# Dilated attention with all four heads of a block in one unit, placed on a common beat in TensorE's order

## The chip, the cores and the metric

The kernel runs on one core of a Trainium2 chip (trn2). The metric is the device time of one execution in microseconds (us). The engines are TensorE (PE in the profile, its weight loads PEld), VectorE (DVE), ScalarE (ACT), GpSimd (POOL) and SyncE (SP, which issues most DMAs). Each engine works through its own instructions in the order in which the program lists them; semaphores hold it where it needs another's result.

## What is computed

The reference is a trunk of two layers for 1024 tokens of width 1024. In each layer a normalised input is projected into a pooling mixer and into queries, keys and values of 12 heads. The heads form three groups of four, each with its own window and dilation:

```
DIL_PATTERNS = ((128, 1), (512, 4), (2048, 16))
def dilated_window_attention(q, k, v, window, dil):      # one group of four heads
    steps = window // dil
    ...                                   # tokens split by residue mod dil, then into blocks of 128
    s = einsum('brnqhd,brnkhd->brnhqk', qs, kb) * HEAD_DIM ** -0.5    # kb: the block and the one before it
    s = where((dist >= 0) & (dist <= steps) & (ki >= 0), s, -inf)
    m = max(s); e = exp(s - m); l = sum(e)
    o = einsum('brnhqk,brnkhd->brnqhd', e / l, vb); lse = m + log(l)
...
    wts = softmax(stack(lses))            # the three groups are weighed against each other
    h = h + concat([pool_out, attn_out]) @ w_out
    h = h + square(relu(rmsnorm(h) @ w_up)) @ w_down
    h = h + sigmoid(rmsnorm(h) @ w_gate) * (p[i] @ w_ple[i])
```

## The kernel before, in words

Everything is float32. The large products split each operand into a high and a low part in a rounded float32 format (fp32r) and add three products of them; `products` (lines 549, 551 and 553) issues these as matmuls of 128x128 weights and 512 columns. For one tile of the input projection that is 8 x 3 such matmuls for each half of the tokens. The attention's own matmuls are plain fp32.

The program is written as a planner: a `Clock` holds a time `now` and a heap of pieces of work with due times. `products` calls `ck.tick` after each matmul, which moves the time on by 215 ns and runs whatever has come due. So the order of each engine's instructions is fixed when the program is built: attention's matmuls land between the products of the next projection, where the plan's time puts them, and `ck.now +=` books what they are thought to cost.

In each layer, groups 0 and 1 project queries (`in_qk`), keys and values (`in_v`), then call `attend`, whose work is laid over the projections that follow: group 0's over the six tiles of group 1, group 1's over the four query and key tiles of group 2. The halves of queries and keys are rotated by `rot_evac` (VectorE shuffles and multiplies, GpSimd multiplies, VectorE adds), and the weights of each next tile are split on ScalarE and VectorE, in the same stretch. Group 2's attention lies over the pooling tiles and the projection of its values.

`unit` (line 763) is one unit of attention: a block of 128 queries and, for groups 0 and 1, two heads (a pair); for group 2, all four heads. In group 0 every block but the first, and in group 1 every second block, sees 256 keys (called wide here: K is 256, nb is 2); all others see 128 (narrow). Its steps:

1. scores: one matmul for each head into the two PSUM banks of tag "s" (line 783). Head 2p + hh sits in rows 64 hh to 64 hh + 63, so these use half of the array's rows;
2. on VectorE mask and maximum of each head (line 789) and the scaling of the maxima (line 793), on ScalarE the exponential of each head with its sum (line 796);
3. `stats_out`: GpSimd issues a DMA with the block's maxima and sums (line 759);
4. transposes of the exponentials, 128x128 each, into a bank of tag "e" (two banks in all; line 805), and their eviction by VectorE or ScalarE in turn (lines 810, 812);
5. values: one matmul for each head and key block into the one bank of tag "o" (line 819); head hh fills 64 columns of the array. ScalarE evicts the result (lines 825, 828, 831).

Each step yields the planned time to the next; the value step also waits in the plan until the values are there (`vok`). `attend` starts a unit every 3400 ns for groups 0 and 1 (16 units each) and every 2500 ns for group 2 (8 units), each running its own course. An fp32 score or value matmul shows in the trace as two instructions, a transpose as one. `weigh` (line 975) waits in the plan for the units' outputs and multiplies them by the weights of the groups, before the output projection.

Of the kernel before, what the change touches and what calls it, by code (L numbers as in the profile page):

```python
# [116 lines left out]
def body(nc, tc, pools, A, out):  # L117
# [6 lines left out]
    def bank(name, tag, shape=(128, 512)):  # L124
        return ps.tile(list(shape), F32, name=name, tag=tag)
# [495 lines left out]
    def layer(L, hT, norm, tabs):  # L621
# [141 lines left out]
        def unit(g, n, ps_, q, k, vget, o, lag):  # L763

            two = (n > 0) if g == 0 else (n % 2 == 1) if g == 1 else False
            nb = 2 if two else 1
            np_ = len(ps_)
            K = 128 * nb
            if g == 2:
                mk = cst[:, C_MASK[2]:C_MASK[2] + 128]  # L770
            else:
                mk = cst[:, C_MASK[g] + 256 - K:C_MASK[g] + 256]
            heads = [(i, hh, 2 * p + hh) for i, p in enumerate(ps_) for hh in range(2)]
            for p in ps_:
                for t in (q[p], k[p]):
                    for hf in range(2):
                        ck.need((id(t), hf))
            sp = [bank(f"s{g}", "s", (128, np_, K)) for _ in range(2)]
            k0 = (n - nb + 1) * 128
            for i, hh, h in heads:  # L780
                r = slice(64 * hh, 64 * hh + 64)
                p = ps_[i]
                nc.tensor.matmul(sp[hh][:, i], q[p][r, n * 128:n * 128 + 128],  # L783
                                 k[p][r, k0:k0 + K], start=True, stop=True)
            ck.now += 218.0 * nb * np_
            yield 350.0
            sm = blk(f"sm{g}", F32, (128, np_, 2, K))
            for i, hh, h in heads:
                nc.vector.tensor_tensor_reduce(sm[:, i, hh], sp[hh][:, i], mk, 1.0, -3.0e38,  # L789
                                               OP.add, OP.max, ml[g][:, n, h:h + 1])  # L790
            nm = small.tile([128, 2 * np_], F32, name="nm", tag="nm", bufs=6)
            h0 = 2 * ps_[0]
            nc.vector.tensor_scalar(nm, ml[g][:, n, h0:h0 + 2 * np_], -0.125, None, op0=OP.mult)  # L793
            yield 500.0 + 300.0 * nb * np_
            for j, (i, hh, h) in enumerate(heads):
                nc.scalar.activation(sm[:, i, hh], sm[:, i, hh], AF.Exp, bias=nm[:, j:j + 1],  # L796
                                     scale=0.125, accum_out=ml[g][:, n, 4 + h:5 + h])
            yield 900.0 * np_ + 300.0
            if ps_[-1] == 1:
                stats_out(g, n)  # L800
            stats[g] += np_
            ep = bank(f"e{g}", "e", (128, np_, 2, nb, 128))
            for i, hh, h in heads:
                for kb in range(nb):
                    nc.tensor.transpose(ep[:, i, hh, kb], sm[:, i, hh, kb * 128:kb * 128 + 128], ident)  # L805
            ck.now += 107.0 * 2 * nb * np_
            yield 300.0
            et = blk(f"et{g}", F32, (128, np_, 2, nb, 128))
            if (n + ps_[0]) % 2:
                nc.vector.tensor_copy(et, ep)  # L810
            else:
                nc.scalar.activation(et, ep, AF.Copy)
            yield 900.0 + lag
            while not all(vok(g, n, p) for p in ps_):
                yield 500.0
            op = bank(f"o{g}", "o", (128, np_, 128))
            for i, hh, h in heads:
                for kb in range(nb):
                    nc.tensor.matmul(op[64 * hh:64 * hh + 64, i], vget(n - nb + 1 + kb, h),  # L819
                                     et[:, i, hh, kb], start=kb == 0, stop=kb == nb - 1)  # L820
            ck.now += 107.0 * 2 * nb * np_
            yield 300.0
            for i, p in enumerate(ps_):
                if g == 0:
                    nc.scalar.activation(o[p].rearrange("p (r n a) -> p n r a", r=8, n=8)[:, n],
                                         op[:, i].rearrange("p (r a) -> p r a", r=8), AF.Copy)
                elif g == 1:
                    nc.scalar.activation(o[p].rearrange("p (s x a) -> p x s a", s=2, x=8)[:, n],
                                         op[:, i].rearrange("p (s a) -> p s a", s=2), AF.Copy)
                else:  # L830
                    nc.scalar.activation(o[p][:, n * 128:n * 128 + 128], op[:, i], AF.Copy)

        def attend(g, q, k, vget, base, gap, lag=0.0):
            o = [blk(f"o{g}{p}_{L}") for p in range(2)]
            oT[g] = o
            i = 0
            for n in range(8):
                for ps_ in (((0, 1),) if g == 2 else ((0,), (1,))):
                    ck.go(unit(g, n, ps_, q, k, vget, o, lag), ("o", g, n, ps_[-1]), base + gap * i)
                    i += 1  # L840
# [692 lines left out]
```

## Time and profile before

| | us |
|---|---|
| median of 3 runs | 2332.04 |
| lowest and highest | 2331.57, 2335.32 |
| profiled execution | 2332.01 |
| its span, first to last instruction | 2330.2 |
| TensorE busy in it | 2280.8 (98%) |
| VectorE, ScalarE, GpSimd busy | 1677.5, 1014.7, 694.3 |

The busy time of TensorE is no measure of distance from its best: matmuls are pipelined and their ends are modelled, so that a late start need not show as idle time. What a run of instructions costs is read from the starts: how much later the next product starts than it would have. A row of the timeline merges neighbouring instructions of one kind and gives their first start, the time to their last end, and their count.

### The profile page before, as it was taken

The page shows a single profiled execution, that of the slowest core. Times are in us where ns is not written, and L with a number is a line of the kernel's source. Part 1 is how long each engine was busy: PE and PEld are TensorE (multiplying, and loading weights), DVE is VectorE, ACT ScalarE, POOL GpSimd, SP SyncE. Part 2 cuts the span into 40 slices and gives each one's busy share as a digit, 9 for nine tenths or more (in the row PEclk, how much of TensorE's full clock was granted, in tenths as well). Part 3 has the DMA queues.
Part 4 walks back from the last instruction along what each step waited for, and adds up shares of the span by engine and source line. Part 5 has one row for each costly group of instructions (what it writes and reads, how often), then busy time and mean ns, then how long its engine had stood idle before and what let it go on. Part 6 is the DMA issues. An engine that isn't in the chain of part 4 may idle for free.

```text
span 2330.2 us, 30901 instructions
## 1 busy us (share of the span) xinstructions
PE 2280.8 (98%) x11088; PEld 1841.8 (79%) x11088; DVE 1677.5 (72%) x2832; ACT 1014.7 (44%) x2147; POOL 694.3 (30%) x538
## 2 busy tenths in 40 slices
PE   8999999999999999999999999999999999999998
PEld 6767788788887788888887767878888877888888
DVE  7555677787778787886565467688777787787845
ACT  5243543433345444354324345434333443434645
POOL 5111136333332232342221122354333323333322
PEclk9999999999999999999999999999999999999999
DMA  5011133254447745432220111433444575545214
GB/s 181 19 38 28 38 92 109 77 171 153 155 150 257 234 136 164 148 95 70 61 59 19 38 38 39 106 112 117 155 156 157 198 237 179 172 127 169 89 55 136
DMA packets 296369, 275.65 MB, mean 118 GB/s; under 512 B 12476, under 2 KB 224056, under 8 KB 296216
## 3 DMA queue, kind: packets, MB, share of 16 engines
q1 hardware_dynamic: 293624, 270.04, 37.3%
q0 software_dynamic: 2272, 3.61, 0.9%
q8 instruction: 87, 1.43, 0.3%
q14 instruction: 66, 0.54, 0.1%
q10 hardware_dynamic: 320, 0.03, 0.0%
HBM read 200.99 MB, written 72.58 MB: 117 GB/s over the span
## 4 chain that ended last, share of the span: by engine, by line
PE 82%; DVE 8%; DMA 3%; POOL 2%; ACT 2%; issue 2%; SPq 0%; DVEq 0%; ACTq 0%; POOLq 0%
PE X L566 27%; PE Z L566 12%; PE Y L566 7%; PE in L551 6%; PE in L549 6%; PE in L553 5%; PE gt L553 2%; PE gt L551 2%; PE gt L549 2%; PE s L783 2%; PE o L819 2%; DVE wP L1230 2%; DMA wP<-x_d 2%; PE e L805 1%; POOL res L1058 1%
## 5 line engine op out<-in xcount | busy, mean ns | idle before, releaser
L1230 DVE TENSOR_TENSOR wP<-wP 128x512 fp32r<-128x512 f32 x252 | 197.5, 808 | 0.9 <-ACT wP L1228 0.9
L566 PE MATMUL X<-wP,d1p 128*128 128x512 f32 x768 | 186.2, 395 | 10.2 <-DVE acc L1242 9.7
L566 PE MATMUL X<-wP,d0p 128*128 128x512 f32 x768 | 186.2, 395 | 10.0 <-DVE acc L1242 9.5
L566 PE MATMUL X<-xP,u0p 128*128 128x512 f32 x768 | 183.2, 391 | 0.4 <-ACT y L1164 0.4
L566 PE MATMUL X<-xP,u1p 128*128 128x512 f32 x768 | 183.1, 391 | 0.4 <-ACT y L1164 0.4
L566 PEld LDWEIGHTS X<-wP,d0p 128*128 128x128 f32 x768 | 145.5, 191 | 44.4 <-DVE acc L1242 6.9
L566 PEld LDWEIGHTS X<-wP,d1p 128*128 128x128 f32 x768 | 145.4, 190 | 44.6 <-DVE acc L1242 7.2
L566 PEld LDWEIGHTS X<-xP,u0p 128*128 128x128 f32 x768 | 144.6, 189 | 30.9 <-ACT y L1164 0.8
L566 PEld LDWEIGHTS X<-xP,u1p 128*128 128x128 f32 x768 | 144.6, 189 | 30.9 <-ACT y L1164 0.8
L1190 ACT ACTIVATE y<-y 128x1024 f32<-128x1024 f32 x64 | 67.5, 1055 | 211.8 <-DVE y L1187 211.8
L1228 ACT ACTIVATE wP<-wP 128x512 fp32r<-128x512 f32 x252 | 147.3, 617 | 24.6 <-DMA wP<-x_d 22.2
L190 DVE SCALAR_TENSOR_TENSOR wl<-wr,gt,wh 128x128 fp32r<-128x128 f32 (+1 forms) x288 | 119.9, 447 | 38.5 <-ACT wh L196 38.3
L678 POOL TENSOR_TENSOR rot<-rot,s 128x512 f32<-128x512 f32 x48 | 61.4, 1284 | 278.6 <-DVE rot L676 217.6
L1242 DVE TENSOR_TENSOR acc<-acc,X 128x512 f32<-128x512 f32 x128 | 87.4, 683 | 77.9 <-PE X L566 63.8
L796 ACT ACTIVATE sm<-sm,nm 128x128 f32<-128x128 f32 (+1 forms) x192 | 84.5, 442 | 93.3 <-DVE nm L793 93.1
L196 ACT ACTIVATE wh<-wr,gt 128x128 fp32r<-128x128 f32 (+1 forms) x304 | 104.3, 396 | 0.5 <-DMA wr<-in_w_in_dram 0.5
L566 PE MATMUL Z<-xP,u0p 128*128 128x512 f32 x384 | 93.5, 393 | 4.6 <-DVE res L1079 4.6
L566 PE MATMUL Z<-xP,u1p 128*128 128x512 f32 x384 | 93.5, 393 | 4.5 <-DVE res L1079 4.5
L789 DVE CUSTOM_DVE_ANT_0 sm<-s,cst 128x128 f32<-128x128 f32 (+1 forms) x192 | 58.3, 347 | 52.1 <-PE s L783 52.0
L566 PE MATMUL Z<-wP,d0p 128*128 128x512 f32 x384 | 91.9, 389 | 0.0
L566 PE MATMUL Z<-wP,d1p 128*128 128x512 f32 x384 | 91.9, 389 | 0.0
L330 ACT ACTIVATE d0p<-d0s 128x512 fp32r<-128x512 f32 x64 | 40.1, 628 | 111.9 <-PE X L566 65.7
(474 smaller groups left out, 5923.8 us busy)
## 6 DMA issues: line engine op xcount, KB each, us to landing
wP<-x_d SPq DMA_DIRECT2D x252, 256.0 KB, 3.6
x_d<-ys SPq DMA_DIRECT2D x64, 512.0 KB, 3.6
wr<-in_w_in_dram SPq DMA_DIRECT2D x40, 512.0 KB, 4.2
u0r<-in_w_up_dram SPq DMA_DIRECT2D x32, 512.0 KB, 5.1
x_d<-y SPq DMA_DIRECT2D x32, 512.0 KB, 2.8
u1r<-in_w_up_dram SPq DMA_DIRECT2D x32, 512.0 KB, 5.4
d0r<-in_w_down_dram SPq DMA_DIRECT2D x28, 512.0 KB, 5.8
d1r<-in_w_down_dram SPq DMA_DIRECT2D x28, 512.0 KB, 5.9
```

The costliest lines, as they stand in the source:

```text
L190: nc.vector.scalar_tensor_tensor(l[:, k], raw[:, k], gs[k], f(h[:, k]), op0=OP.mult, op1=OP.subtract)
L196: nc.scalar.activation(h[:, k], raw[:, k], AF.Copy, scale=gs[k])
L549: nc.tensor.matmul(p, wh, h[:, cols], start=first and i == 0, stop=False)
L551: nc.tensor.matmul(p, wh, l[:, cols], start=False, stop=False)
L553: nc.tensor.matmul(p, wl, h[:, cols], start=False, stop=last and i == n - 1)
L566: nc.tensor.matmul(p, w[:, a, i], x[:, b], start=first and i == 0 and a == b == 0, stop=i == n - 1 and a == 1, skip_group_check=not first)
L678: nc.gpsimd.tensor_tensor(a, a, tb["s"][:, hs(hf)], op=OP.mult)
L796: nc.scalar.activation(sm[:, i, hh], sm[:, i, hh], AF.Exp, bias=nm[:, j:j + 1], scale=0.125, accum_out=ml[g][:, n, 4 + h:5 + h])
L1190: nc.scalar.activation(y, y, AF.Square)
L1228: nc.scalar.activation(t[:, 0], f(t[:, 1]), AF.Copy)
L1230: nc.vector.tensor_tensor(t[:, 1], f(t[:, 1]), f(t[:, 0]), op=OP.subtract)
L1242: nc.vector.tensor_tensor(a, a, p, op=OP.add)
```

## The change

A unit of groups 0 and 1 takes all four heads of a block, as group 2's does: 8 units for each group instead of 16. `Unit` holds the steps as methods. `beats` issues them: every 5900 ns of plan, one after the other without a product between them, the transposes of the unit made a beat ago, the values of the one made two beats ago, and the scores of a new one; a group has ten beats. Group 2 keeps its 2500 ns; there the transposes are those of two beats ago and stand directly ahead of the new scores, and the values follow on their own (`alone`). For a wide unit the transposes fill both banks of tag "e", evicted one by VectorE and one by ScalarE; a narrow one fills one bank and is evicted once. The maxima of four heads are scaled by one instruction instead of two. `stats_out` is called together with the exponentials instead of 1200 ns of plan later. `weigh` waits for the unit of four heads.

```diff
-        def unit(g, n, ps_, q, k, vget, o, lag):
-            two = (n > 0) if g == 0 else (n % 2 == 1) if g == 1 else False
...
-            yield 900.0 * np_ + 300.0
-            if ps_[-1] == 1:
-                stats_out(g, n)
...
+        class Unit:
+            def __init__(self, g, n, q, k, vget, o):
+                self.g, self.n, self.q, self.k, self.vget, self.o = g, n, q, k, vget, o
+                two = (n > 0) if g == 0 else (n % 2 == 1) if g == 1 else False
+                self.nb = 2 if two else 1
+                self.heads = [(p, hh, 2 * p + hh) for p in range(2) for hh in range(2)]
+                ck.waiting.add(("o", g, n, 1))
+
+            def scores(self):
...
+                self.sp = [bank(f"s{g}", "s", (128, 2, K)) for _ in range(2)]
+                k0 = (n - self.nb + 1) * 128
+                for p, hh, h in self.heads:
+                    r = slice(64 * hh, 64 * hh + 64)
+                    nc.tensor.matmul(self.sp[hh][:, p], self.q[p][r, n * 128:n * 128 + 128],
+                                     self.k[p][r, k0:k0 + K], start=True, stop=True)
+                ck.now += 436.0 * self.nb
+                ck.go(self.softmax(), delay=350.0)
+
+            def softmax(self):
...
+                self.sm = blk(f"sm{g}", F32, (128, 2, 2, K))
+                for p, hh, h in self.heads:
+                    nc.vector.tensor_tensor_reduce(self.sm[:, p, hh], self.sp[hh][:, p], mk, 1.0, -3.0e38,
+                                                   OP.add, OP.max, ml[g][:, n, h:h + 1])
+                nm = small.tile([128, 4], F32, name="nm", tag="nm", bufs=6)
+                nc.vector.tensor_scalar(nm, ml[g][:, n, 0:4], -0.125, None, op0=OP.mult)
+                yield 500.0 + 600.0 * self.nb
+                for p, hh, h in self.heads:
+                    nc.scalar.activation(self.sm[:, p, hh], self.sm[:, p, hh], AF.Exp, bias=nm[:, h:h + 1],
+                                         scale=0.125, accum_out=ml[g][:, n, 4 + h:5 + h])
                 stats_out(g, n)
+                stats[g] += 2
+
+            def turn(self):
+                g, nb = self.g, self.nb
+                self.ep = ([bank(f"e{g}", "e", (128, 2, nb, 128)) for _ in range(2)] if nb == 2 else
+                           [bank(f"e{g}", "e", (128, 2, 2, 1, 128))])
+                self.et = blk(f"et{g}", F32, (128, 2, 2, nb, 128))
+                for p, hh, h in self.heads:
+                    for kb in range(nb):
+                        d = self.ep[p][:, hh, kb] if nb == 2 else self.ep[0][:, p, hh, kb]
+                        nc.tensor.transpose(d, self.sm[:, p, hh, kb * 128:kb * 128 + 128], ident)
+                ck.now += 428.0 * nb
+                ck.go(self.copy(), delay=300.0)
+
+            def copy(self):
+                for p, e in enumerate(self.ep):
+                    d = self.et[:, p] if self.nb == 2 else self.et
+                    if (self.n + p) % 2:
+                        nc.vector.tensor_copy(d, e)
+                    else:
+                        nc.scalar.activation(d, e, AF.Copy)
+                return
+                yield
+
+            def mix(self):
+                g, n, nb = self.g, self.n, self.nb
+                op = bank(f"o{g}", "o", (128, 2, 128))
+                for p, hh, h in self.heads:
+                    for kb in range(nb):
+                        nc.tensor.matmul(op[64 * hh:64 * hh + 64, p], self.vget(n - nb + 1 + kb, h),
+                                         self.et[:, p, hh, kb], start=kb == 0, stop=kb == nb - 1)
+                ck.now += 428.0 * nb
+                ck.go(self.out(op), ("o", g, n, 1), 300.0)
...
-        def attend(g, q, k, vget, base, gap, lag=0.0):
+        def attend(g, q, k, vget, base, gap, late):
             o = [blk(f"o{g}{p}_{L}") for p in range(2)]
             oT[g] = o
-            i = 0
-            for n in range(8):
-                for ps_ in (((0, 1),) if g == 2 else ((0,), (1,))):
-                    ck.go(unit(g, n, ps_, q, k, vget, o, lag), ("o", g, n, ps_[-1]), base + gap * i)
-                    i += 1
+            units = [Unit(g, n, q, k, vget, o) for n in range(8)]
+
+            def alone(u):
+                yield 1500.0
+                while not vok(g, u.n, 0):
+                    yield 500.0
+                u.mix()
+
+            def beats():
+                t = ck.now
+                for i in range(8 + 2 * late):
+                    if 0 <= i - late < 8:
+                        u = units[i - late]
+                        u.turn()
+                        if g == 2:
+                            ck.go(alone(u))
+                    if g < 2 and i >= 2 * late:
+                        u = units[i - 2 * late]
+                        while not (vok(g, u.n, 0) and vok(g, u.n, 1)):
+                            yield 500.0
+                        u.mix()
+                    if i < 8:
+                        units[i].scores()
+                    t += gap
+                    yield max(100.0, t - ck.now)
+            ck.go(beats(), delay=base)
...
             attend(g, q, k, lambda n, h, v=v: v[h // 2][:, n, 64 * (h % 2):64 * (h % 2) + 64],
-                   5000.0, 3400.0)
+                   5000.0, 5900.0, 1)
...
         attend(2, q, k, lambda n, h: v2[n // 4][:, n % 4, 64 * h:64 * h + 64],
-               3500.0, 2500.0)
+               3500.0, 2500.0, 2)
...
-                keys.add(("o", g, n, 1 if g == 2 else p))
+                keys.add(("o", g, n, 1))
```

## Rows read from the trace of the kernel before

**Rows 1.** TensorE's waits, 95 to 345 us: line, waited for, us, times, longest

```profile
PE o L819 <- DVE et L810: 0.8, 1, 0.8
```

**Rows 2.** Windows of projection matmuls: stretch, us, busy (instructions), clock, DMA, GB/s

```profile
94.60:168.00 73.40, 50.25 (x180) 1.00 0.14 38
194.80:262.60 67.80, 52.02 (x184) 1.00 0.17 34
```

**Rows 3.** TensorE timeline, group 0: start us, us, engine line operation shapes count

```profile
114.47 0.40 PE L553 MATMUL in<-h_0H,wl 128*128 128x512 f32 x1
114.70 0.40 PE L549 MATMUL in<-h_1H,wh 128*128 128x512 f32 x1
115.03 0.66 PE L819 MATMUL o<-et,v 128*64 128x128 f32 x8
...
115.96 0.39 PE L553 MATMUL in<-h_1H,wl 128*128 128x512 f32 x1
...
116.51 0.70 PE L783 MATMUL s<-k,q 64*128 64x256 f32 x4
...
117.87 0.39 PE L553 MATMUL in<-h_2H,wl 128*128 128x512 f32 x1
```

**Rows 4.** TensorE timeline, group 1, narrow and wide pairs

```profile
216.49 0.49 PE L783 MATMUL s<-k,q 64*128 64x128 f32 x4
...
217.25 0.39 PE L553 MATMUL in<-h_2H,wl 128*128 128x512 f32 x1
...
218.27 0.44 PE L819 MATMUL o<-et,v 128*64 128x128 f32 x4
...
218.97 0.39 PE L551 MATMUL in<-h_4L,wh 128*128 128x512 f32 x1
...
220.91 0.70 PE L783 MATMUL s<-k,q 64*128 64x256 f32 x4
...
221.88 0.39 PE L549 MATMUL in<-h_7H,wh 128*128 128x512 f32 x1
```

**Rows 5.** TensorE timeline, units of four heads of group 2

```profile
266.62 0.67 PE L819 MATMUL o<-et,v 128*64 128x128 f32 x8
267.22 0.71 PE L783 MATMUL s<-k,q 64*128 64x128 f32 x8
...
268.20 0.39 PE L551 MATMUL in<-h_6L,wh 128*128 128x512 f32 x1
...
269.13 0.60 PE L805 MATMUL e<-cst,sm 128*128 128x128 f32 x4
...
269.80 0.39 PE L549 MATMUL in<-h_0H,wh 128*128 128x512 f32 x1
270.12 0.72 PE L783 MATMUL s<-k,q 64*128 64x128 f32 x8
...
271.11 0.40 PE L553 MATMUL in<-h_0H,wl 128*128 128x512 f32 x1
...
275.41 0.60 PE L805 MATMUL e<-cst,sm 128*128 128x128 f32 x4
...
276.92 0.40 PE L551 MATMUL in<-h_5L,wh 128*128 128x512 f32 x1
```

**Rows 6.** Timeline of all engines, one wide pair: scores to exponentials

```profile
120.84 0.70 PE L783 MATMUL s<-k,q 64*128 64x256 f32 x4
...
121.57 0.42 DVE L789 CUSTOM_DVE_ANT_0 sm<-s,cst 128x256 f32<-128x256 f32 x1 [3.08 <-PE s L783]
...
121.92 0.42 DVE L789 CUSTOM_DVE_ANT_0 sm<-s,cst 128x256 f32<-128x256 f32 x1
...
122.65 0.51 ACT L796 ACTIVATE sm<-sm,nm 128x256 f32<-128x256 f32 x1 [2.30 <-DVE nm L793]
```

**Rows 7.** GpSimd by line, 94.6 to 262.6 us: count, busy us, mean ns

```profile
L759 POOL DMA_DIRECT2D st_d<-ml x15 | 11.0, 731 | 45.5 <-ACT wh L196 16.9 <-ACT sm L796 10.5 <-ACT o L825 9.8
```

**Rows 8.** Window, all engines, after TensorE idled: us, busy (instructions), clock, DMA

```profile
420.00:424.00 4.00, 1.69 (x4) 1.44 (x5) 3.81 (x6) 0.72 (x2) 0.00 (x0) 0.50 0.00 0
```

More of the change, by code (lines that the diff above doesn't have):

```diff
@@ L761, in stats_out @@
                 nc.gpsimd.dma_start(out=mlp[g], in_=st_d[g].rearrange("(t c) e -> c t e", c=128))
-        def unit(g, n, ps_, q, k, vget, o, lag):
-            two = (n > 0) if g == 0 else (n % 2 == 1) if g == 1 else False
[L766 to L797, printed above, removed]
-            yield 900.0 * np_ + 300.0
-            if ps_[-1] == 1:
-                stats_out(g, n)
[L801 to L831, printed above, removed]
@@ L833, in attend, with out @@
-        def attend(g, q, k, vget, base, gap, lag=0.0):
+        class Unit:
[6 more added lines that the diff above has]
+            def scores(self):
+                g, n, K = self.g, self.n, 128 * self.nb
+                for p in range(2):
+                    for t in (self.q[p], self.k[p]):
+                        for hf in range(2):
+                            ck.need((id(t), hf))
+                self.sp = [bank(f"s{g}", "s", (128, 2, K)) for _ in range(2)]
[7 more added lines that the diff above has]
+            def softmax(self):
+                g, n, K = self.g, self.n, 128 * self.nb
+                if g == 2:
+                    mk = cst[:, C_MASK[2]:C_MASK[2] + 128]
+                else:
+                    mk = cst[:, C_MASK[g] + 256 - K:C_MASK[g] + 256]
+                self.sm = blk(f"sm{g}", F32, (128, 2, 2, K))
[8 more added lines that the diff above has]
+                                         scale=0.125, accum_out=ml[g][:, n, 4 + h:5 + h])
+                stats_out(g, n)
+                stats[g] += 2
[15 more added lines that the diff above has]
+                        nc.vector.tensor_copy(d, e)
+                    else:
+                        nc.scalar.activation(d, e, AF.Copy)
[10 more added lines that the diff above has]
+                ck.go(self.out(op), ("o", g, n, 1), 300.0)
+            def out(self, op):
+                g, n, o = self.g, self.n, self.o
+                for p in range(2):
+                    if g == 0:
+                        nc.scalar.activation(o[p].rearrange("p (r n a) -> p n r a", r=8, n=8)[:, n],
+                                             op[:, p].rearrange("p (r a) -> p r a", r=8), AF.Copy)
+                    elif g == 1:
+                        nc.scalar.activation(o[p].rearrange("p (s x a) -> p x s a", s=2, x=8)[:, n],
+                                             op[:, p].rearrange("p (s a) -> p s a", s=2), AF.Copy)
+                    else:
+                        nc.scalar.activation(o[p][:, n * 128:n * 128 + 128], op[:, p], AF.Copy)
+                return
+                yield
@@ L834, in attend @@
+        def attend(g, q, k, vget, base, gap, late):
             o = [blk(f"o{g}{p}_{L}") for p in range(2)]
             oT[g] = o
-            i = 0
-            for n in range(8):
-                for ps_ in (((0, 1),) if g == 2 else ((0,), (1,))):
-                    ck.go(unit(g, n, ps_, q, k, vget, o, lag), ("o", g, n, ps_[-1]), base + gap * i)
-                    i += 1
+            units = [Unit(g, n, q, k, vget, o) for n in range(8)]
[10 more added lines that the diff above has]
+                        u.turn()
+                        if g == 2:
+                            ck.go(alone(u))
[9 more added lines that the diff above has]
+            ck.go(beats(), delay=base)
```

## The prediction, made before the change was run

> **What bounds the kernel now.** I read the waits first, then the windows, then TensorE's order row by row. In the stretch from 95 to 345 us, where the first layer projects queries, keys and values and attends between them, TensorE waits for another engine once, 0.8 us [rows 1]; the second layer answers with the same single row. So the stage is bound by TensorE's own order: what counts is how long the small attention runs hold up the row of 512-column products, and no other engine ends last. The windows with only the products counted show how much that is: in the 73.4 us of head group 0 there are 180 products, and in the 67.8 us of group 1 there are 184 [rows 2]. Between the runs a product starts every 0.23 us (114.47 to 114.70 [rows 3]). That leaves 73.4 - 180 x 0.23 = 32.0 us for attention in group 0 and 67.8 - 184 x 0.23 = 25.5 us in group 1. One unit's last transposes and the last two value runs of group 1 lie outside its window; they are 0.44, 0.80 and 0.59 us by the prices below, together 27.3 us.
>
> **What one run costs.** Take the second product after a run, less the run's start. A run of scores or values starts 0.33 us after the product before it (114.70 to 115.03 [rows 3]) where a product would follow after 0.23, and the first product after it is also late; the run's price is that difference plus 0.33 less two undisturbed steps of 0.23, so the difference less 0.13. A run of transposes starts 0.23 after its product: difference less 0.23.
> - Eight values: 115.96 - 115.03 - 0.13 = 0.80 [rows 3]. Four values: 218.97 - 218.27 - 0.13 = 0.57 [rows 4]. So 0.058 an instruction, and 0.34 fixed.
> - Four narrow scores (128 columns): 217.25 - 216.49 - 0.13 = 0.63 [rows 4]; eight: 271.11 - 270.12 - 0.13 = 0.86 [rows 5]. So 0.058 each, 0.40 fixed. Four wide scores: 221.88 - 220.91 - 0.13 = 0.84 [rows 4], so 0.11 each.
> - Four transposes: 269.80 - 269.13 - 0.23 = 0.44 [rows 5]: 0.11 each, and nothing fixed.
> - Values and scores side by side: 268.20 - 266.62 - 0.13 = 1.45 for eight and eight [rows 5], where 0.80 + 0.86 = 1.66 would be due apart. The junction saves 0.21.
> - Four wide scores with four transposes behind them: 117.87 - 116.51 - 0.13 = 1.23 [rows 3] against 0.84 + 0.44 = 1.28: saves 0.05.
>
> So scores and values each pay about 0.4 and 0.34 us for entering and leaving, whatever the length of the run, and transposes pay nothing.
>
> **The change part by part, for groups 0 and 1 of one layer.** The instructions on TensorE stay the same, each fp32 product of scores and values being two of them: for group 0 60 transposes, 120 values and 64 scores (56 wide), for group 1 48, 96 and 64 (32 wide). What changes is the number of runs. Before, each of 16 pair units has one run of scores and one of values; after, 8 beats have scores and 8 have values, and in 6 of the 10 beats of a group the two stand side by side.
> - Group 0 after: 60 x 0.11 + 120 x 0.058 + 56 x 0.11 + 8 x 0.058 = 20.2 us of instructions; 8 x (0.40 + 0.34) - 6 x 0.21 = 4.7 us fixed. Together 24.9 against 32.0: 7.1 us saved.
> - Group 1 after: 48 x 0.11 + 96 x 0.058 + 32 x 0.11 + 32 x 0.058 = 16.2, and 4.7 fixed: 20.9 against 27.3, 6.4 us saved.
> - Two layers: 27.0 us. All of it is on the path, since nothing else ends last in the stage.
>
> No row shows transposes directly ahead of values. The nearest are scores ahead of transposes, which save 0.05 [rows 3], and transposes ahead of scores, which save 0.02 [rows 5]; I take nothing, and 28 such junctions at 0.05 would give 1.4 us more. The Trainium skill (TensorEngine Tiling (Array Packing), Key Properties) says that a change of tiling mode drains the engine while a change of tile does not; by that rule full-array transposes next to 64-column values gain nothing either.
>
> Group 2 keeps its units of four heads and its separate values; its transposes move directly ahead of another unit's scores: 276.92 - 275.41 - 0.23 = 1.28 us together [rows 5], 0.44 + 0.86 = 1.30 apart, so nothing there. ScalarE's and VectorE's work hardly changes: half as many scalings of the maxima, one eviction of 512 columns where two of 256 were, and off the path by [rows 1].
>
> **What is late next.** A beat is planned at 5900 ns, of which the planner books 2584 for a wide unit's TensorE work; the other 3316 at 215 each are 15.4 products, on the chip 3.55 us. The next beat opens with the transposes of the scores just made, so their softmax has to be over by then. Its chain by [rows 6]: the first maximum starts 0.73 us after four wide scores begin, so 1.17 after eight; four maxima at 0.35, then the scaling and the first exponential 0.73 after the start of the last maximum (121.92 to 122.65), four exponentials at 0.51: 1.17 + 1.05 + 0.73 + 2.04 = 5.0 us. The last head's transposes are due after some 1.1 us of scores, 3.55 of products and 0.66 of the other heads' transposes: 5.3 us. That is 0.3 us of slack; a pair, with half the maxima and exponentials, has a chain of 0.73 + 0.35 + 0.73 + 1.02 = 2.8 us by the same rows. Rotary work on VectorE and weight splitting on ScalarE share these queues, so some of the 22 wide units of both layers will be late. The trace has no such wait; below it is bounded by nothing, above by a VectorE queue late by 0.85 us in each, 22 x 0.55 = 12 us. I take 2 us, nearest to the 0.8 us per layer that TensorE waits now.
>
> One more wait is added. The statistics' DMA now is queued on GpSimd together with the exponentials, not 1.2 us of plan later. It stands there until the exponentials end, with the rotary multiplication behind it; VectorE's addition waits for that, and the next unit's maxima stand behind the addition. The next maxima are a whole beat away, so I cost it at nothing; without that cover it is a rival.
>
> Sum: the profiled execution took 2332.0 us (2330.2 of span and 1.8 around it), the median is the same. 2332.0 - 27.0 + 2.0 = 2307.0 us.
>
> **The rivals.**
> 1. Late softmax. If VectorE and ScalarE are behind by 0.6 to 1.2 us in every wide beat, TensorE stands 0.3 to 0.9 us before the last transposes: 22 x that is 7 to 20 us, 2312 to 2325. For it: the slack of 0.3 us. Against: nothing in the stage waits for an exponential now [rows 1].
> 2. Slower through GpSimd. The statistics' wait (up to 2 us of exponentials and 0.73 us of issue [rows 7]) pushes a rotary multiplication, so an addition, so the maxima of the next unit. 16 halves of queries and keys are rotated within the two groups of a layer. If each pushes its beat by 2.7 us less 0.3 of slack, 32 x 2.4 = 77 us are lost: some 2382. It decides from a mean push of 27 / 32 + 0.3 = 1.1 us. Against: a beat is 3.55 + 3.2 = 6.8 us, and the addition is done before the next maxima unless both fall late.
> 3. The fixed costs don't go. If they belong to a pair of heads and not to a run, sixteen values cost two times eight, and only the number of instructions counts: 2332. Against: eight scores or values cost less than two times four, in each kind [rows 3 to 5].
> 4. The clock. A beat puts about 3.2 us of small fp32 work in one place. After TensorE stood idle the granted clock fell to the lower level in the trace (0.50, that is 1.2 GHz [rows 8]), while it is 1.00 through all attention now [rows 2]. Should each of the 24 beats with all three kinds cost as little as 4 us at 1.2 GHz, half of that time lost, it is 48 us: 2355. Against: runs of 1.23 us [rows 3] lie in a window whose clock is 1.00 [rows 2]. The Trainium skill (TensorE: Matmul & The Clock Gate, A second HAM failure mode) tells of a kernel whose clock rose and fell since TensorE paused briefly between groups of matmuls; no run here shows that in attention.
>
> **How the numbers follow.** The forecast, 2300 to 2312 with 2307 as its value, has 0.76; rival 1 0.12, rival 2 0.05, rival 3 0.04, rival 4 0.03. The low end is no stall, the 1.4 us of junctions, and 3 us for falls of the clock elsewhere that last a different time. The range goes up over half of rival 1 to 2318. A difference of 0.2% (4.7 us) is about what a measurement can tell from none: faster 0.88, same 0.04, slower 0.08.
>
> **What would show it.** Right: in TensorE's order of group 0 runs of eight transposes, sixteen values and eight scores with 15 or 16 products between them, the next but one product 3.2 us plus 0.46 after the one before; elapsed time for the same products of group 0 smaller by some 7 us; no wait for an exponential over a few tenths. Wrong: waits of transposes for ScalarE of half a microsecond and more in most beats, a granted clock under 1.00 between 95 and 250 us, or sixteen values that cost 1.6 us.

## The result and the profile after

| | before | after |
|---|---|---|
| median of 4 runs, us | 2332.31 | 2307.23 |
| lowest and highest | 2331.57, 2335.32 | 2303.73, 2308.21 |
| ratio, 95% interval | | 0.9881, 0.9869 to 0.9893 |
| profiled execution | 2332.01 | 2306.82 |
| its span | 2330.2 | 2305.1 |

The median fell by 25.1 us; 2307.0 had been forecast.

The clearest view is one window for each kernel, from the first score of the first layer to the first product of the output projection. Columns: stretch, its length, busy us with instruction counts of TensorE, its weight loads, VectorE, ScalarE and GpSimd, then the granted clock, the DMA share and GB/s. Before:

```profile
95.01:327.00 231.99, 231.15 (x1379) 168.00 (x1379) 148.63 (x471) 108.42 (x375) 46.02 (x45) 1.00 0.19 45
```

After:

```profile
95.27:313.50 218.23, 217.76 (x1379) 174.63 (x1379) 139.60 (x451) 107.55 (x374) 45.86 (x45) 1.00 0.20 48
```

The same 1379 instructions of TensorE, busy from end to end at a clock of 1.00 in both, now take 13.8 us less: the work is the same, but fewer runs pay for an entry. The second layer's stage (1238.65 to 1470.6 before, 1226.90 to 1445.1 after) shrinks from 232.0 to 218.2 us, by the same amount. In the first layer group 0 alone gave 7.5 us: from the product ahead of its first score to the 183rd behind it, 94.69 to 169.18 us became 94.95 to 161.96.

One beat of group 0 in TensorE's timeline, the answer to [rows 3] (start us, us, engine, line, operation, shapes, count; line 815 is the transposes, 834 the values, 783 the scores):

```profile
115.46 0.40 PE L549 MATMUL in<-h_4H,wh 128*128 128x512 f32 x1
115.70 1.04 PE L815 MATMUL e<-cst,sm 128*128 128x128 f32 x8
116.67 1.14 PE L834 MATMUL o<-et,v 128*64 128x128 f32 x16
117.74 1.13 PE L783 MATMUL s<-k,q 64*128 64x256 f32 x8
118.80 0.50 PE L551 MATMUL in<-h_4L,wh 128*128 128x512 f32 x1
119.14 0.40 PE L553 MATMUL in<-h_4H,wl 128*128 128x512 f32 x1
```

From the product before the beat to the second one behind it are 119.14 - 115.46 = 3.68 us, of which two undisturbed steps are 0.46; the beat costs 3.21 to 3.22 us. The prediction named 3.2, with 15 or 16 products to the next beat, and that is what stands there: the next three beats begin behind products at 122.15, 129.02 and 135.66.

TensorE's waits between 95 and 345 us, the answer to [rows 1] (line, waited for, us, times, longest):

```profile
PE o L834 <- ACT v L1056: 0.3, 1, 0.3
```

No wait for an exponential reaches this list; the single one of [rows 1], for VectorE's eviction of transposes, has gone. Of GpSimd, from 94.6 to 262.6 us, the answer to [rows 7]:

```profile
L759 POOL DMA_DIRECT2D st_d<-ml x16 | 11.8, 736 | 40.2 <-ACT wh L196 27.5 <-DVE rot L677 6.7 <-ACT sm L802 5.5
```

**Where the forecast's size was off.** Each run of the first layer is priced from the start of the product ahead of it to the second product behind it, less two undisturbed steps of 0.228 us. The prices sum as follows (us; group 1's last transposes and values, which stand beside runs of group 2, are counted with group 1; group 2 without its last value run, which starts behind the window):

| one layer | before, forecast | before, trace | after, forecast | after, trace |
|---|---|---|---|---|
| group 0 | 32.0 | 32.4 | 24.9, and 0.5 of stalls | 25.2 |
| group 1 | 27.3 | 27.5 | 20.9, and 0.5 of stalls | 21.1 |
| group 2 | unchanged | 16.3 | unchanged | 16.6 |

That is 13.7 us less for the runs of groups 0 and 1, and the window shows 13.8. Two small terms cancel. Group 2 pays 0.4 more, nearly all of it where one value run waits for ScalarE (the row of waits above). And some 0.4 us are gained in the steps behind the runs: from the second to the seventh step behind a run a product takes 229 to 233 ns on average where later ones take 227, and there are fewer runs. Two layers save 27.5 us in the two windows, where 25.0 had been forecast (27.0 less 2.0 of stalls). The span shrank by 25.1: outside the windows 2.3 us were lost again (0.3 ahead of the first, 1.75 between the two, 0.3 behind the second).

**Where 2.3 us went back.** Between the windows stand the output projection and the layer's later products, which the change does not touch. There TensorE waits, as before, for a sum of VectorE, and around the end of that wait the granted clock falls. Timeline rows of such a wait, before and then after:

```profile
741.24 4.38 PE L566 MATMUL X<-wP,d0p 128*128 128x512 f32 x12 [5.09 <-DVE acc L1242]
```

```profile
727.48 5.46 PE L566 MATMUL X<-wP,d0p 128*128 128x512 f32 x12 [5.32 <-DVE acc L1284]
```

The same 12 products take 4.38 us and then 5.46. The windows of 5 us around this wait and the next one, of 3.2 and 3.1 us (columns as above), show the clock. Before:

```profile
740.00:745.00 5.00, 3.76 (x11) 3.04 (x12) 4.60 (x6) 1.89 (x5) 2.76 (x2) 0.66 1.04 404
745.00:750.00 5.00, 5.00 (x23) 4.13 (x22) 4.79 (x9) 4.12 (x8) 0.00 (x0) 1.00 1.16 328
...
785.00:790.00 5.00, 5.00 (x16) 3.93 (x15) 4.52 (x8) 2.71 (x5) 0.00 (x0) 0.66 0.86 226
790.00:795.00 5.00, 5.00 (x23) 4.13 (x22) 3.31 (x6) 0.63 (x1) 0.00 (x0) 1.00 0.60 213
```

After:

```profile
725.00:730.00 5.00, 2.52 (x6) 2.07 (x7) 3.35 (x4) 2.04 (x5) 3.22 (x3) 0.62 1.04 409
730.00:735.00 5.00, 5.00 (x17) 3.98 (x17) 3.95 (x8) 4.64 (x10) 0.00 (x0) 0.70 1.13 340
...
770.00:775.00 5.00, 3.27 (x8) 2.60 (x9) 4.02 (x7) 3.02 (x6) 1.65 (x2) 0.56 1.12 337
775.00:780.00 5.00, 5.00 (x19) 4.00 (x18) 2.78 (x5) 0.65 (x2) 0.00 (x0) 0.76 0.48 139
```

At the lower of its two levels, 1.2 GHz, the engine's clock stands for (1 - 0.66) / 0.5 x 5 = 3.4 us around the end of each of the two waits before, and for (0.38 + 0.30) / 0.5 x 5 = 6.8 us at the first of them after, the same sum at the second. Set product against product, these two places cost 2.3 us, and 0.5 us came back at an earlier fall between the windows. That this need not come with the change shows in the eleven profiled executions of this study: the stretch between the two windows, the same code in all of them, takes from 909.9 us (e9, with the change's units and beats) to 915.5, and 914.4 in a second execution of the change. A kernel's two attention windows agree within 0.2 us in all but one.

So the total came out at 25 us by two errors that cancel: 2.5 us more saved in the stage than forecast, 2.3 us lost outside it. That the median met 2307.0 within 0.3 us is luck; that the stage saved 27.5 us where 25.0 were forecast is not.

### The profile page after: what moved, and what is told of

Same layout as the page of the kernel before. It is cut to its first block, busy times and chain, and to the rows that moved or that the text cites. A ratio compares the mean times of both kernels' runs of the same rounds, so it can differ in the third digit from the quotient of the medians.

```text
span 2305.1 us, 30864 instructions
## 1 busy us (share of the span) xinstructions
PE 2256.4 (98%) x11088; PEld 1857.6 (81%) x11088; DVE 1654.5 (72%) x2790; ACT 1013.6 (44%) x2147; POOL 695.5 (30%) x538
## 4 chain that ended last, share of the span: by engine, by line
PE 81%; DVE 9%; DMA 3%; ACT 3%; POOL 2%; issue 2%; SPq 0%; DVEq 0%; ACTq 0%; POOLq 0%
PE X L566 27%; PE Z L566 12%; PE Y L566 7%; PE in L551 5%; PE in L553 5%; PE in L549 5%; PE gt L551 3%; PE gt L553 3%; PE gt L549 3%; DVE wP L1272 2%; PE o L834 2%; PE s L783 2%; DMA wP<-x_d 2%; POOL res L1100 1%; DMA acc<-h_d 1%
## 5 line engine op out<-in xcount | busy, mean ns | idle before, releaser
L566 PE MATMUL X<-wP,d0p 128*128 128x512 f32 x768 | 188.2, 398 | 10.1 <-DVE acc L1284 9.6
L330 ACT ACTIVATE d1p<-d1s 128x512 fp32r<-128x512 f32 x64 | 40.1, 628 | 111.7 <-PE X L566 65.5
```

Source lines behind the costliest of these rows:

```text
L330: nc.scalar.activation(t[:, 0], src, AF.Copy)
L566: nc.tensor.matmul(p, w[:, a, i], x[:, b], start=first and i == 0 and a == b == 0, stop=i == n - 1 and a == 1, skip_group_check=not first)
```

## The experiments

A kernel's attention window (first score to first product of the output projection, us, first and second layer) is the sharper measure; its median carries the falls of the clock too. The kernel before was measured again beside each set of experiments, and the ratios are to that: its median was 2335.04 us beside e1 to e4, 2333.53 beside e5 to e8, and one run of 2330.78 stood beside e9.

| kernel | median | ratio to before, 95% | windows |
|---|---|---|---|
| before | 2332.31 | | 232.0, 232.0 |
| the change | 2307.23 | 0.9869 to 0.9893 | 218.2, 218.2 |
| e1 runs apart | 2328.62 | 0.9964 to 0.9983 | 228.4, 228.3 |
| e2 pairs on the beat | 2324.76 | 0.9945 to 0.9976 | 227.3, 227.3 |
| e3 values first | 2309.30 | 0.9872 to 0.9910 | 219.1, 219.1 |
| e4 transposes last | 2300.99 | 0.9845 to 0.9874 | 215.9, 215.9 |
| e5 e4 with runs apart | 2308.92 | 0.9878 to 0.9908 | 219.4, 219.4 |
| e6 e4, group 2 by two blocks | 2298.11 | 0.9827 to 0.9857 | 212.9, 213.0 |
| e7 the change again | 2307.84 | 0.9873 to 0.9906 | 218.2, 218.2 |
| e8 values twice | 2331.88 (1 run) | | 230.0, 230.0 |
| e9 statistics later | 2305.68 (1 run) | | 218.9, 219.3 |

### What does standing side by side give? (e1_apart, e5_apart_late)

Theory: nearly all the gain is fewer entries, and the neighbours give only the 0.21 us of each junction of values and scores. Rival: the three kinds must stand together for the gain. e1 puts a product or two between the three runs of each beat (`ready` is set when the plan has issued the unit's exponentials):

```diff
                         u = units[i - late]
+                        while not u.ready:
+                            yield 50.0
                         u.turn()
...
                         u = units[i - 2 * late]
+                        yield 400.0
...
                     if i < 8:
+                        if g < 2:
+                            yield 400.0
                         units[i].scores()
```

> The changed kernel with the three steps of a beat in groups 0 and 1 kept apart by two products or so: same units of four heads, same number of score runs (48) and value runs (48), but no run of values directly ahead of scores. Theory (a fixed cost for each run of scores, 0.40 us, or of values, 0.34 us, of which 0.21 us is saved where the two stand side by side): only the 24 junctions of 0.21 us are lost, so 5.0 us more than 2307.2, 2312.2 us, and the first product of the output projection starts 2.5 us later than 313.5. Rival (standing together is what gains): the gain is lost, some 2330 us. Rival (the units of four heads alone gain): 2307 us.

It lost 10.2 and 10.1 us in the two windows, four times what the theory allowed. The runs themselves cost what they cost alone (sixteen values 1.28 us, eight wide scores 1.27), so the junctions explain 2.5. The rest is a wait, which both had left out. One wide unit of e1, VectorE, ScalarE and TensorE (lines in e1: 784 scores, 676 and 677 rotary work, 797 maxima, 803 exponentials, 817 transposes; in brackets the idle time before and what ended it):

```profile
111.30 1.13 PE L784 MATMUL s<-k,q 64*128 64x256 f32 x8
...
112.91 0.74 DVE L676 STREAM_SHUFFLE rot<-in 128x512 f32<-128x512 f32 x1
...
113.54 0.67 DVE L677 TENSOR_TENSOR rot<-in,c 128x512 f32<-128x512 f32 x1
...
114.13 0.41 DVE L797 CUSTOM_DVE_ANT_0 sm<-s,cst 128x256 f32<-128x256 f32 x1
...
115.82 0.51 ACT L803 ACTIVATE sm<-sm,nm 128x256 f32<-128x256 f32 x1 [3.98 <-DVE nm L800]
...
116.48 1.91 PE L817 MATMUL e<-cst,sm 128*128 128x128 f32 x8 [0.64 <-ACT sm L803]
```

The gaps use up products of the beat: from the second wide unit of a group on, 11 to 14 of them stand between its scores and its transposes, 15 to 18 in the change. In this unit there are 14, and rotary work stands ahead of the maxima, which start 2.83 us after the scores; the transposes begin 5.2 us after them, when the second exponential has only started. Five of the seven wide units of group 0 have only 11 or 12, and their transposes come too early even where nothing delays the maxima. The transposes above last 1.91 us instead of 1.04 (115.70 above), and the list of TensorE's waits between 60 and 400 us has a new first row:

```profile
PE e L817 <- ACT sm L803: 1.8, 3, 0.6
PE o L836 <- ACT v L1063: 0.3, 1, 0.3
```

The list counts only time in which TensorE is shown idle; the runs of eight transposes, priced from start to start, cost between 0.88 and 2.56 us where 0.88 is due, and one run of four 2.06 where 0.44 is; in one layer this makes 8.5 us above what is due. With the junctions (2.5) and less the 0.65 us of late transposes that the change has already (below), that makes 10.3 against the 10.2 measured. The sum was argued only, since e1 moves two things at once. So e5 separates the runs where the exponentials can't be late, with the transposes last in the beat:

```diff
+                    if g == 2 and i < 8:
+                        units[i].scores()
...
-                    if 0 <= i - late < 8:
-                        u = units[i - late]
-                        u.turn()
...
                         u.mix()
-                    if i < 8:
+                        yield 400.0
+                    if g < 2 and i < 8:
                         units[i].scores()
+                        yield 400.0
+                    if 0 <= i - late < 8:
+                        u = units[i - late]
+                        u.turn()
```

> The kernel with transposes last (e4), its three steps in groups 0 and 1 kept apart by two products or so. As in e1 no small runs stand side by side there, but the transposes now come after the scores, so their softmax has time. Theory A (in e1 the runs themselves cost what the separate runs do, and the rest of its loss is transposes waiting for exponentials): against e4 24 junctions of values and scores at 0.205 us and 28 of scores and transposes at 0.044 us are lost, 6.1 us: 2307.1 us, first product of the output projection 3.1 us later than 310.7, no wait of transposes for ScalarE. Theory B (standing together itself gains what e1 lost): some 2325 us, and 11 us later.

Window 219.4 against 215.9 for the same order without gaps (e4, below): 3.4 us lost, 3.1 expected by theory A. In e5's waits no exponential appears:

```profile
PE o L834 <- ACT v L1060: 0.4, 1, 0.4
```

Standing apart costs the junctions and 0.3 us more; the slightly longer steps behind a run, now behind 24 more of them, could be that, which is not shown. The rest of e1's loss was the softmax.

### Number of runs, or number of instructions? (e2_pairs, e8_values_twice)

e2 keeps the beat and the order but gives a unit one pair again: two beats of half the size, of 2950 ns.

```diff
-            units = [Unit(g, n, q, k, vget, o) for n in range(8)]
+            units = [Unit(g, n, ps_, q, k, vget, o) for n in range(8)
+                     for ps_ in (((0, 1),) if g == 2 else ((0,), (1,)))]
...
-                   5000.0, 5900.0, 1)
+                   5000.0, 2950.0, 2)
```

> Pairs of heads again in groups 0 and 1, but on a beat of half the length, transposes, values and scores together (transposes two beats late, values four): 80 runs of scores and 80 of values instead of 48 and 48, 48 junctions of values and scores instead of 24. Theory (fixed cost for each run): 32 x 0.40 + 32 x 0.34 - 24 x 0.21 = 18.6 us more than 2307.2, 2325.8 us; first product of the output projection 9.3 us later than 313.5. Rival (standing together is what gains, whatever the size of the unit): 2307 us.

Its windows are 9.1 and 9.0 us longer than the change's, 9.3 expected. Its wide beat:

```profile
116.30 0.39 PE L549 MATMUL in<-h_4H,wh 128*128 128x512 f32 x1
116.53 0.60 PE L816 MATMUL e<-cst,sm 128*128 128x128 f32 x4
117.06 0.67 PE L833 MATMUL o<-et,v 128*64 128x128 f32 x8
117.66 0.70 PE L784 MATMUL s<-k,q 64*128 64x256 f32 x4
...
118.62 0.39 PE L553 MATMUL in<-h_4H,wl 128*128 128x512 f32 x1
```

118.62 - 116.30 - 0.46 = 1.86 us, and twice that is 3.72 where the four heads cost 3.21: half a microsecond in each full beat for the same instructions. That is the end of the prediction's third rival: the fixed part belongs to the run.

e8 does the opposite: as many runs, but each value product of groups 0 and 1 issued twice, the second time over the first result.

```diff
-                for p, hh, h in self.heads:
+                for p, hh, h in self.heads * (2 if g < 2 else 1):
```

> The changed kernel with every value matmul of groups 0 and 1 issued twice into the same place, one run behind the other without a gap: 432 instructions more in the same 32 runs. Theory (0.058 us an instruction inside a run, the entry paid once): 25.1 us more than 2307.2, 2332.3 us, first product of the output projection 12.5 us later than 313.5. Rival (each instruction carries its share of 0.10 us of a run of eight): 43 us more, 2350 us.

```profile
115.52 0.39 PE L549 MATMUL in<-h_4H,wh 128*128 128x512 f32 x1
...
116.72 2.02 PE L834 MATMUL o<-et,v 128*64 128x128 f32 x32
118.66 1.14 PE L783 MATMUL s<-k,q 64*128 64x256 f32 x8
...
120.07 0.40 PE L553 MATMUL in<-h_4H,wl 128*128 128x512 f32 x1
```

120.07 - 115.52 - 0.46 = 4.09 us, 0.87 above the change's beat, for 16 instructions more: 0.055 each, where the prediction had 0.058 from eight against four. The windows grew by 11.8 us, 12.5 expected.

### Which order of the three? (e3_values_first, e4_transposes_last)

e3 issues values, transposes, scores; e4 values, scores, transposes. The edit of e3, and behind it that of e4 against e3:

```diff
-                    if 0 <= i - late < 8:
-                        u = units[i - late]
-                        u.turn()
...
                         u.mix()
+                    if 0 <= i - late < 8:
+                        u = units[i - late]
+                        u.turn()
...
                     if i < 8:
                         units[i].scores()
```

```diff
+                    if i < 8:
+                        units[i].scores()
                     if 0 <= i - late < 8:
                         u = units[i - late]
                         u.turn()
...
-                    if i < 8:
-                        units[i].scores()
```

> Within a beat the order is values, transposes, scores, so that transposes stand between the two; the same number of runs as in the changed kernel. Theory (transposes use the array as products do, so values and scores no longer share an entry): 24 x 0.21 = 5.0 us more, 2312.2 us, first product of the output projection 2.5 us later than 313.5. Rival (any neighbour among the small matmuls saves the entry): 2307 us.

> Within a beat the order is values, scores, transposes. Values and scores stay side by side; 40 runs of transposes come directly behind scores, which saved 0.05 us in the trace of the kernel before: 2.0 us less, 2305.2 us, first product of the output projection 1.0 us earlier than 313.5. The transposes come some 2 us later after their softmax, so its slack grows from 0.3 to over 2 us: no wait of transposes for ScalarE. Rival (the place of the transposes is free): 2307 us.

A full beat of e3, then of e4:

```profile
115.07 0.39 PE L549 MATMUL in<-h_4H,wh 128*128 128x512 f32 x1
115.39 1.15 PE L834 MATMUL o<-et,v 128*64 128x128 f32 x16
116.46 1.09 PE L815 MATMUL e<-cst,sm 128*128 128x128 f32 x8
117.49 1.14 PE L783 MATMUL s<-k,q 64*128 64x256 f32 x8
...
118.89 0.40 PE L553 MATMUL in<-h_4H,wl 128*128 128x512 f32 x1
```

```profile
114.53 0.39 PE L549 MATMUL in<-h_4H,wh 128*128 128x512 f32 x1
114.85 1.14 PE L834 MATMUL o<-et,v 128*64 128x128 f32 x16
115.93 1.13 PE L783 MATMUL s<-k,q 64*128 64x256 f32 x8
116.99 1.09 PE L815 MATMUL e<-cst,sm 128*128 128x128 f32 x8
...
118.16 0.39 PE L553 MATMUL in<-h_4H,wl 128*128 128x512 f32 x1
```

They cost 3.36 and 3.17 us, against 3.21 in the order of the change. e3 loses the 0.21 of the junction of values and scores and wins 0.04 by transposes behind values, 0.15 to 0.17 net. e4 keeps the 0.21 and wins 0.04 by transposes behind scores. Both gained something else: the first wide unit of groups 0 and 1 was no longer late, since its transposes come 1 to 2 us later in the beat. In e4 the first beat of group 0 with all three kinds costs 2.68 us, 3.09 in the change. And e4 loses another lateness: the last transposes of group 2 begin at 278.41 in the change, while their unit's exponentials still run, and cost 0.96 us; they cost 0.96 before as well, and 0.44 in e4. So the windows moved by +0.9 for e3 (theory +2.5, which did not have the wait in it) and by -2.3 for e4 (-1.0 expected, short for the same reason). e4 is faster than the change by 6 us of median; of that 4.6 are the two windows.

### Does the place of the statistics' DMA cost anything? (e9_statistics_later)

```diff
                                          scale=0.125, accum_out=ml[g][:, n, 4 + h:5 + h])
+                yield 2100.0
                 stats_out(g, n)
```

> The changed kernel with the statistics' DMA queued on GpSimd 2.1 us of plan behind the exponentials, as before, so that GpSimd no longer stands in front of unfinished exponentials with a rotary multiplication behind it. Theory (that wait costs nothing, the next maxima are a whole beat away; the 0.3 us that the first wide unit of groups 0 and 1 still loses come from VectorE's own order): first product of the output projection at 313.5 us, within 0.1. Rival 2 of the prediction (the wait delays the next unit's maxima): earlier by some tenths for each unit that is late now, up to 0.7 us.

The windows became longer, by 0.7 and 1.1 us, which neither theory had: the rival expected the opposite sign. Beat for beat, groups 0 and 1 take the same times as in the change within 10 ns, so the early DMA costs nothing there. What grew lies in group 2: value runs there waited for ScalarE's eviction of the values projected just ahead of them (row of e9's timeline, then the one of the change):

```profile
311.72 0.66 PE L835 MATMUL o<-et,v 128*64 128x128 f32 x8 [0.89 <-ACT v L1057]
```

```profile
306.49 0.66 PE L834 MATMUL o<-et,v 128*64 128x128 f32 x8 [0.28 <-ACT v L1056]
```

The two rows are different runs of group 2, the longest such wait in each kernel. That the delay moved later work of the plan against those evictions is inferred, not shown. The second layer of e9 has two such waits, 1.3 us in sum, against one of 0.3 in the change. The second rival's mechanism did not occur in groups 0 and 1.

### The same step once more (e6_two_units, e7_changed_again)

If a run's entry is what costs, group 2 has runs to save too. e6 takes e4 and does two blocks of group 2 at once: eight transposes, sixteen scores, sixteen values in one run each, in shared banks (`alone2` puts both blocks' values into one).

```diff
+            def twos():
...
+                for i in range(5):
+                    if i < 4:
+                        sp = [bank(f"s{g}", "s", (128, 4, 128)) for _ in range(2)]
+                        for j in range(2):
+                            units[2 * i + j].scores([s[:, 2 * j:2 * j + 2] for s in sp])
+                    if i:
+                        a, b = units[2 * i - 2:2 * i]
+                        a.turn()
+                        b.turn()
+                        ck.go(alone2(a, b))
...
-            ck.go(beats(), delay=base)
+            ck.go(twos() if g == 2 else beats(), delay=base)
```

> The kernel with transposes last (e4), and in group 2 two blocks at a time: one run of sixteen narrow scores with sixteen... eight transposes behind them, and one run of sixteen values, so 8 runs of scores and 8 of values fewer in two layers. Theory (fixed cost for each run): 8 x 0.40 + 8 x 0.34 less 6 junctions of scores and transposes at 0.05 = 5.6 us less than e4's 2301.0: 2295.4 us, first product of the output projection 2.8 us earlier than 310.7. Rival (group 2's values lie between products of 256 columns and its last pair delays the weighing): no gain, 2301 us or more.

> The changed kernel once more, beside e6 on the same chip. 2307 us; its runs differ by some 2 us as the stretches of lower granted clock in the later stages differ in length; the first product of the output projection at 313.5 us.

e6 is the fastest kernel of the study: 2298.11 us, 0.9842 of before, and 9.7 us under the change, which ran beside it as e7 (2307.84). Its window is 3.0 us shorter than e4's; a part of that is one value run that now stands behind the window's end, and up to the last product of line 549 in the output projection (279.2 us after the first score, 281.4 in e4) it is 2.2 us in each layer, 2.8 expected. In e6 a product of the pooling (`pm`, line 966) waits 0.6 us in each layer, which e4 has not; e4's wait of a value run for ScalarE, 0.3 us, is gone. A run of sixteen narrow scores costs 1.30 us in it where two of eight cost 0.85 each. e7 shows how well the window repeats: 218.2 again in both layers, while between its windows it took 914.4 us, the change 913.4.

## Why the prediction was right, point by point

**The bound.** Right. The stage is TensorE's own order: of the 218 us, lateness that prices show adds up to 1.5 us (0.34 and 0.31 in the first wide units below, 0.5 in group 2's last transposes, 0.35 in one value run). The list of waits names only the last, so it alone does not prove that nothing waits.

**The price of a run.** Right, and the strongest step. The fixed 0.34 and 0.40 us by which a value and a score run are entered and left do not grow with four heads instead of two (e2, e8). The 0.21 of the junction is in the beat: eight transposes and sixteen values cost 2.15 us, eight wide scores 1.27 alone (e5), and the beat 3.21 instead of 3.42. The sums for after, 24.9 and 20.9 us, met 24.8 and 20.8 (25.2 and 21.1 less the two late beats).

**What before cost.** Mis-sized, by 0.4 us in group 0 and 0.2 in group 1. The prediction subtracted 180 and 184 products at 0.23 us. In the trace after, 16 undisturbed steps from the product at 111.81 to that at 115.46 take 3.65, 0.228 each; rounding up made 180 steps 0.4 us too long and attention so much too cheap in group 0. The 0.8 us wait of [rows 1] was inside the 32.0 us, though the prediction did not say so, and it did go.

**The junctions with no row.** Transposes ahead of values were taken at nothing, with 1.4 us as the bound. Nothing was right: eight transposes with sixteen values cost 2.15 us, and 8 x 0.11 + 1.27 is 2.15. In the other direction e3 has 2.11. The Trainium skill (TensorEngine Tiling (Array Packing), Key Properties) says that changing the tiling mode drains TensorE. That runs of another tile form pay for an entry, and full-array transposes do not, agrees with it, but the runs show that the changes are not equal: from 64-column values to 64-row scores 0.21 us are saved, from either to full-array transposes 0.04 to 0.05, from transposes to values none.

**The softmax slack.** Estimated at 0.3 us, with a chain of 5.0 us. In the change the chain from the first score to the end of the last exponential takes 4.86 to 4.93 us where nothing stands in front of it: scores at 117.74 above, and

```profile
118.90 0.42 DVE L796 CUSTOM_DVE_ANT_0 sm<-s,cst 128x256 f32<-128x256 f32 x1 [1.40 <-PE s L783]
...
120.61 0.51 ACT L802 ACTIVATE sm<-sm,nm 128x256 f32<-128x256 f32 x1 [2.32 <-DVE nm L799]
...
122.11 0.49 ACT L802 ACTIVATE sm<-sm,nm 128x256 f32<-128x256 f32 x1
```

The first maximum starts 1.16 us after the scores (1.17 forecast [rows 6]), the last exponential ends at 122.60. In these units the last head's transposes start 0.3 to 1.1 us after its exponential ends. The stalls, 2 us in the forecast, were 1.3: not spread over 22 units, but in the first wide unit of each of groups 0 and 1, 0.34 and 0.31 us in each layer. The cause is an order on VectorE that the prediction did not look for. Rows of that unit of group 0:

```profile
102.51 1.14 PE L783 MATMUL s<-k,q 64*128 64x256 f32 x8
...
104.35 0.01 DVE L676 LOAD_MASK_SELECT rot<-in  x1 [3.49 <-PE in L553]
104.35 0.73 DVE L676 STREAM_SHUFFLE rot<-in 128x512 f32<-128x512 f32 x1
...
104.97 0.67 DVE L677 TENSOR_TENSOR rot<-in,c 128x512 f32<-128x512 f32 x1
...
105.56 0.41 DVE L796 CUSTOM_DVE_ANT_0 sm<-s,cst 128x256 f32<-128x256 f32 x1
...
107.32 0.51 ACT L802 ACTIVATE sm<-sm,nm 128x256 f32<-128x256 f32 x1 [3.52 <-DVE nm L799]
```

The rotary shuffle stands ahead of the maxima in VectorE's queue and waits for the last product of its tile, which on TensorE stands behind the scores. So the maxima start 3.05 us after the scores instead of 1.16, and this unit's transposes, at 108.49, last 1.40 us instead of 1.04.

**The rivals.** The late softmax is real, but it begins past the slack: e1, with 11 to 14 products to the transposes, pays 8.5 us a layer for it. About four products less, 0.9 us, were enough. GpSimd's statistics: no cost in the beats of groups 0 and 1, where e9 has them later and the beats take the same times. Fixed costs that stay: refuted by e2 and e8. The clock: 1.00 over the whole window above, with beats of 3.2 us of small fp32 work in it; the falls are where they were, at waits of 3.0 to 5.3 us in later stages, but for one at the execution's end.

**The range.** 3 us for falls of a different length elsewhere stood only at its low end; between the windows they went the other way, by 1.75 us, and belong on both sides.

## What to carry to other kernels

Where small matmuls of another tile form are strewn between large ones, price the entry of a run and not the instruction: read the second large product after the run, subtract two undisturbed steps, and compare runs of different length. Then gather runs until the results they wait for become late, and find that point in the queue of the engine that makes them, since one instruction there that waits for a later product turns hidden work into a stall. Judge such an edit by a window with the same instruction count in both kernels, as the whole time can move by some microseconds for reasons elsewhere.

## What the runs showed of the hardware

- The order of two neighbouring runs matters in one direction: transposes behind values save 0.04 us and behind scores 0.05, transposes ahead of values nothing. The order with the transposes last costs 3.17 us a full beat, the change's 3.21, with them in the middle 3.36.
- The fp32 value instruction takes 0.055 us inside a run of 32, and 16 narrow scores cost 1.30 us: by the prices from before these would be 0.058 and 0.40 + 16 x 0.058 = 1.33, so the price stays nearly linear beyond the lengths in that trace.
- At the same waits of TensorE, 1.2 GHz lasted 3.4 us in one execution and 6.8 in another, with the same products. Over a profiled execution, without the last stretch in which it ends, these stretches sum to 27 us before and 31 after, and to between 24 (e9) and 38 (e1) in the experiments.
